# Other starting offsets for the six split-weight buffers of a decoder block

## The chip, the cores and the metric

One core of a Trainium2 chip runs the whole layer in one launch. The metric is the device time of one execution in microseconds (us); before the change the median of three runs is 985.9 us (984.83 to 986.01).

## What is computed

One decoder layer on 512 tokens of width 1024, in float32. Cut to what matters here:

```python
z = rmsnorm(h, g_mix) @ w_in                      # 1024 -> 7168: q, k, v, u, two gates
attn_d = dilated_attention(q, k, v) @ w_attn_proj # 12 heads of 128 in three groups
y = gelu(s5_ssm(u, ...))
ssm_d = (y @ w_glu_a) * sigmoid(y @ w_glu_b)
h = h + (gate_attn * attn_d + gate_ssm * ssm_d) @ w_out
n2 = rmsnorm(h, g_ffn)
h = h + (silu(n2 @ w_ffn_gate) * (n2 @ w_ffn_up)) @ w_ffn_down   # 2816 wide
h = h + sigmoid(h @ w_ple_gate) * (p @ w_ple_proj)
out = rmsnorm(h, g_final)
```

## The kernel before

Every large product is made of three TensorE matmuls on float32r operands. A weight w is split into a high part (`whi`, the value rounded to float32r) and a low part (`wlo`, what is left), an activation likewise, and `mm3` (L312 to L316) issues high by high (L314), high by low (L315) and low by high (L316). In a matmul one operand is loaded into the array first (the stationary one, `lhsT`, at most 128 columns; the profile has this load as PEld) and the other is streamed past it (the moving one, `rhs`, up to 512 columns).

The weights come in 162 chunks of up to 128 x 1024 floats, in a fixed order (`PLAN`, then the merge, output, FFN and final projections). `Weights.dma` loads chunk i into one of four `raw` buffers. `Weights.split` (L192) takes it from there: ScalarE casts it into `whi` (L204), VectorE subtracts to get `wlo` (L205), and the loads are topped up. There are three `whi` and three `wlo` buffers of 1024 floats per partition in the pool `wpool`, taken in turn, so chunk i uses buffer i mod 3; the last four chunks have four buffers each of their own in the pool `L6`. `gemm` (L318) goes over the k blocks of a chunk and calls the next split after its fourth block.

In most products the weights are stationary (128 x 128) and an activation tile of 512 columns moves: `xn` (normalised input), then `at` and `yt` (attention and state-space outputs), `mT` (merged), `h1g` (FFN input), `act` (FFN middle). In the others the weights move and the activation is stationary: the v projections (chunks 0, 1, 6, 7 and 34 to 37, with `xn`, 256 columns), `pp` (chunks 136 and 137, with `pT`, 512 columns) and `pg` (chunks 154 to 161, with `h2`, 256 columns).

Order of work: input transposes and v; then the `w_in` products with the attention and state-space work of VectorE, ScalarE and GpSimd woven between them; merge (`at`, `yt`); output projection (`mT`); the two FFN halves, each `h1g` then `act`; the final gate `pg` with the last normalisation.

Where the tiles begin, in bytes from the start of a partition, as the built program has it, with the remainder by 64 in brackets:

| tile | before |
|---|---|
| `whi` buffers 0, 1, 2 | 42432 [0], 46528 [0], 50624 [0] |
| `wlo` buffers 0, 1, 2 | 54720 [0], 58816 [0], 62912 [0] |
| `xn`, `mT`, `h2` (one place) | 67008 [0] |
| `h1g` | 103872 [0] |
| `at` | 126400 [0] |
| `pT` | 140736 [0] |
| `act` | 159712 [32] |
| `yt` | 174048 [32] |

The parts of a tile that one matmul takes lie 512, 1024 or 2048 bytes apart, so the remainder holds for all of them. By 512, `whi`, `wlo`, `xn`, `mT`, `h2`, `h1g`, `at` and `pT` all have the remainder 448, and `act` and `yt` 480.

Of the kernel before, what the change touches and what calls it, by code (L numbers as in the profile page):

```python
# [11 lines left out]
F32R = mybir.dt.float32r  # L12
# [5 lines left out]
P = 128  # L18
# [17 lines left out]
SLOT = 1024  # L36
# [42 lines left out]
def kernel(  # L79
# [21 lines left out]
    class Engine:  # L101


        def __init__(self, eng, fixed, per, per1):
            self.eng, self.fixed, self.per, self.per1 = eng, fixed, per, per1
            self.free, self.func = 0.0, None
# [49 lines left out]
    def nm(s):  # L156
        uid[0] += 1
        return f"{s}_{uid[0]}"
# [11 lines left out]
    keys = []  # L170
    RAW_BUFS, HL_BUFS = 4, 3

    class Weights:
        def __init__(self):
            self.raw = {}
# [16 lines left out]
        def split(self):  # L192
            i = self.ns
            self.ns += 1
            while self.nd <= i:
                self.dma()
            _, nk, n = chunks[i].shape
            sz = nk * n
            t = self.raw.pop(i)
            end = i >= len(chunks) - 4  # L200
            wp = L6 if end else wpool
            hi = wp.tile([P, SLOT], F32R, tag="whi", name=nm("whi"), bufs=4 if end else HL_BUFS)
            lo = wp.tile([P, SLOT], F32R, tag="wlo", name=nm("wlo"), bufs=4 if end else HL_BUFS)
            sca.copy(hi[:, :sz], t[:, :sz])  # L204
            dve.tensor_sub(lo[:, :sz], t[:, :sz], hi[:, :sz].bitcast(F32))  # L205
            self.hl[i] = tuple(w[:, :sz].rearrange("p (k n) -> p k n", n=n) for w in (hi, lo))
            while self.nd < min(i + 1 + RAW_BUFS, len(chunks)):
                self.dma()
# [1189 lines left out]
```

## Time and profile before

| | |
|---|---|
| median of three runs | 985.9 us (984.83 to 986.01) |
| the profiled execution | 984.2 us, of which its span is 982.4 us |
| mean granted TensorE clock | 0.977 |
| PE busy | 938.5 us (96%), 4764 matmuls |
| PEld busy (weight loads) | 796.7 us (81%) |
| DVE, ACT, POOL busy | 553.3, 318.1, 267.6 us |
| DMA | 97.91 MB, mean 100 GB/s |

Busy time of PE counts modelled ends of pipelined matmuls. How fast TensorE goes is therefore read from the distance between the starts of neighbouring matmuls, not from their durations, and a stage in which PE never sits idle is paced by those distances.

### The profile page before, as it was taken

What the parts mean: (1) busy time and instruction counts of PE and PEld (TensorE: products, weight loads), DVE (VectorE), ACT (ScalarE), POOL (GpSimd) and SP (SyncE); (2) the same over time, 40 slices, a digit from 0 to 9 for tenths busy, and PEclk for the clock granted to TensorE, in tenths of its full rate; (3) what the DMA queues carried; (4) which work ended last, traced back from release to release, by engine and by line L of the source; (5) the groups of instructions that cost most, each with busy time, mean ns of one, the idle gap of its engine ahead of it and who ended that gap; (6) DMA issues with size and microseconds to landing.
All of it is one profiled execution on the core that took longest, in us unless ns stands there. A gap on an engine that the chain in (4) does not pass through costs nothing.

```text
span 982.4 us, 12129 instructions
## 1 busy us (share of the span) xinstructions
PE 938.5 (96%) x4764; PEld 796.7 (81%) x4764; DVE 553.3 (56%) x800; ACT 318.1 (32%) x461; POOL 267.6 (27%) x341
## 2 busy tenths in 40 slices
PE   8798969998999999999999999999999999999995
PEld 8687858777889888888888888888888888888895
DVE  6757887886756577345667543343333444334465
ACT  4432214323422323433333332332222233332343
POOL 3759964963710100100025211110001111100025
PEclk9899979999999999999999999999999999999998
DMA  8656323343243235223343233223343322233302
GB/s 225 189 153 84 87 65 81 77 98 83 84 114 86 66 90 168 86 95 98 86 127 109 86 108 107 86 62 100 96 129 97 96 86 88 60 110 108 115 15 86
DMA packets 172984, 97.91 MB, mean 100 GB/s; under 512 B 20544, under 2 KB 168160, under 8 KB 172928
## 3 DMA queue, kind: packets, MB, share of 16 engines
q1 hardware_dynamic: 161840, 91.34, 32.6%
q10 hardware_dynamic: 10752, 4.76, 2.3%
q0 software_dynamic: 336, 1.05, 0.3%
q8 instruction: 37, 0.61, 0.3%
q14 instruction: 19, 0.16, 0.1%
HBM read 90.34 MB, written 6.78 MB: 99 GB/s over the span
## 4 chain that ended last, share of the span: by engine, by line
PE 67%; DVE 3%; POOL 2%; ACT 2%; DMA 1%; issue 1%; ACTq 0%; DVEq 0%; POOLq 0%
PE mm L314 16%; PE mm L316 16%; PE mm L315 16%; PE aux L314 6%; PE aux L316 6%; PE aux L315 6%; PE aux L306 2%; DMA Bp<-ks 1%; POOL fst L121 1%; PE aux L310 1%; DVE sg L121 1%; DVE late L121 1%; ACT jk L121 1%; POOL mx L121 0%; DVE wlo L121 0%
## 5 line engine op out<-in xcount | busy, mean ns | idle before, releaser
L121 DVE TENSOR_TENSOR wlo<-raw,whi 128x1024 fp32r<-128x1024 f32 (+2 forms) x162 | 196.8, 1218 | 157.6 <-ACT whi L121 156.6
L121 ACT CAST whi<-raw 128x1024 fp32r<-128x1024 f32 (+2 forms) x162 | 160.3, 995 | 216.8 <-PE mm L315 112.4
L314 PE MATMUL mm<-xn,whi 128*128 128x512 f32 x384 | 155.2, 404 | 0.0
L316 PE MATMUL mm<-xn,wlo 128*128 128x512 f32 x384 | 152.2, 396 | 3.0 <-DVE wlo L121 3.0
L315 PE MATMUL mm<-xn,whi 128*128 128x512 f32 x384 | 152.0, 396 | 0.0
L121 POOL TENSOR_TENSOR tg<-tg,tu 128x512 f32<-128x512 f32 x22 | 28.3, 1285 | 273.8 <-DVE tu L121 262.4
L316 PEld LDWEIGHTS mm<-xn,wlo 128*128 128x128 f32 x384 | 73.5, 191 | 19.5 <-DVE wlo L121 3.7
L314 PEld LDWEIGHTS mm<-xn,whi 128*128 128x128 f32 x384 | 74.0, 193 | 14.7 <-issue 0.2
L315 PEld LDWEIGHTS mm<-xn,whi 128*128 128x128 f32 x384 | 73.8, 192 | 14.4
L314 PE MATMUL mm<-act,whi 128*128 128x512 f32 x176 | 69.5, 395 | 0.0
L316 PE MATMUL mm<-act,wlo 128*128 128x512 f32 x176 | 69.5, 395 | 0.0
L315 PE MATMUL mm<-act,whi 128*128 128x512 f32 x176 | 69.5, 395 | 0.0
L314 PE MATMUL mm<-h1g,whi 128*128 128x512 f32 x176 | 68.9, 392 | 0.0
L314 PE MATMUL aux<-h1g,whi 128*128 128x512 f32 x176 | 68.6, 390 | 0.0
L316 PE MATMUL mm<-h1g,wlo 128*128 128x512 f32 x176 | 68.5, 389 | 0.0
L315 PE MATMUL mm<-h1g,whi 128*128 128x512 f32 x176 | 68.5, 389 | 0.0
L316 PE MATMUL aux<-h1g,wlo 128*128 128x512 f32 x176 | 68.5, 389 | 0.0
L315 PE MATMUL aux<-h1g,whi 128*128 128x512 f32 x176 | 68.5, 389 | 0.0
L121 DVE TENSOR_TENSOR tu<-aux,rs 128x512 f32<-128x512 f32 x22 | 15.2, 691 | 57.4 <-PE aux L316 57.4
L121 ACT CAST act<-tg 128x512 fp32r<-128x512 f32 x22 | 13.7, 621 | 90.6 <-POOL tg L121 90.6
L121 DVE TENSOR_TENSOR act<-tg,act 128x512 fp32r<-128x512 f32 x22 | 15.2, 693 | 47.6 <-ACT act L121 47.6
L121 ACT ACT_TABLE_LOAD x21 | 26.9, 1283 | 41.0 <-PE aux L306 20.1
(243 smaller groups left out, 1869.9 us busy)
## 6 DMA issues: line engine op xcount, KB each, us to landing
raw<-in_w_in_dram SPq DMA_DIRECT2D x56, 512.0 KB, 3.8
raw<-in_w_ffn_gate_dram SPq DMA_DIRECT2D x22, 512.0 KB, 3.8
raw<-in_w_ffn_up_dram SPq DMA_DIRECT2D x22, 512.0 KB, 3.9
raw<-in_w_ffn_down_dram SPq DMA_DIRECT2D x16, 384.0 KB, 3.5
raw<-in_w_ffn_down_dram SPq DMA_DIRECT2D x16, 320.0 KB, 3.3
raw<-in_w_out_dram SPq DMA_DIRECT2D x8, 512.0 KB, 4.6
raw<-in_w_ple_gate_dram SPq DMA_DIRECT2D x8, 512.0 KB, 3.5
xT_d<-xTs SPq DMA_DIRECT2D x4, 512.0 KB, 6.3
```

Of the source, the lines that this page charges most:

```text
L121: return fn(dst, *args, **kw)
L306: nc.tensor.matmul(ps, lhsT=lhsT, rhs=rhs, start=start, stop=stop)
L310: nc.tensor.transpose(ps, src, ident[:n, :n])
L314: nc.tensor.matmul(ps, lhsT=lh, rhs=rh, start=start, stop=False)
L315: nc.tensor.matmul(ps, lhsT=lh, rhs=rl, start=False, stop=False)
L316: nc.tensor.matmul(ps, lhsT=ll, rhs=rh, start=False, stop=stop)
```

## The change

Each buffer is 64 floats longer, each of the six has a tag of its own with one buffer in place of a tag with three, and the part of it that is used begins at another offset: 0, 4 and 8 floats into the three `whi`, 64, 32 and 16 floats into the three `wlo`. The four pairs of `L6` follow the same table by i mod 3.

```diff
+    HOMES = ((0, 64), (4, 32), (8, 16))
...
-            hi = wp.tile([P, SLOT], F32R, tag="whi", name=nm("whi"), bufs=4 if end else HL_BUFS)
-            lo = wp.tile([P, SLOT], F32R, tag="wlo", name=nm("wlo"), bufs=4 if end else HL_BUFS)
+            hb, lb = ("whi", "wlo") if end else (f"whi{i % 3}", f"wlo{i % 3}")
+            hi = wp.tile([P, SLOT + 64], F32R, tag=hb, name=nm("whi"), bufs=4 if end else 1)
+            lo = wp.tile([P, SLOT + 64], F32R, tag=lb, name=nm("wlo"), bufs=4 if end else 1)
+            ho, lw = HOMES[i % 3]
+            hi, lo = hi[:, ho:], lo[:, lw:]
             sca.copy(hi[:, :sz], t[:, :sz])
             dve.tensor_sub(lo[:, :sz], t[:, :sz], hi[:, :sz].bitcast(F32))
```

On every engine the instructions, their order, their shapes and the semaphores they wait for are the same in both programs; only addresses differ. Where the used part of each tile begins now:

| tile | after |
|---|---|
| `whi` buffers 0, 1, 2 | 42432 [0], 51152 [16], 59872 [32] |
| `wlo` buffers 0, 1, 2 | 47040 [0], 55616 [0], 64256 [0] |
| `xn`, `mT`, `h2` | 68544 [0] |
| `h1g`, `at`, `pT` | 105408 [0], 127936 [0], 142272 [0] |
| `act`, `yt` | 159712 [32], 174048 [32], as before |

The `raw` buffers stay where they were. By 512, `whi` has the remainders 448, 464 and 480, `wlo` 448, 320 and 256; the activation tiles keep 448 and 480.

## Rows read from the trace of the kernel before

**Rows 1.** Stretches: length, busy us of PE, PEld, DVE, ACT, POOL, clock, DMA, GB/s
```profile
0.00:30.00 30.00, 22.98 (x153) 22.02 (x153) 18.20 (x22) 14.11 (x21) 14.33 (x17) 0.94 0.92 243
...
60.00:110.00 50.00, 46.98 (x257) 40.62 (x256) 33.98 (x75) 15.34 (x23) 41.81 (x105) 0.97 0.52 101
...
260.00:370.00 110.00, 108.17 (x651) 95.85 (x650) 70.91 (x111) 32.09 (x40) 17.00 (x14) 1.00 0.33 93
...
480.00:720.00 240.00, 240.00 (x1056) 196.85 (x1055) 114.90 (x138) 69.78 (x88) 37.11 (x31) 1.00 0.34 98
...
800.00:930.00 130.00, 130.00 (x598) 107.37 (x597) 50.85 (x61) 40.43 (x56) 6.43 (x5) 1.00 0.32 98
```
**Rows 2.** The same view for PE alone, in the last product (`pg`) and v stretches
```profile
297.30:303.10 5.80, 5.80 (x50) 1.00 0.34 93
306.80:325.00 18.20, 18.20 (x155) 1.00 0.30 87
850.00:860.90 10.90, 10.90 (x50) 1.00 0.12 35
922.60:971.60 49.00, 49.00 (x414) 1.00 0.16 54
```
**Rows 3.** Who waited for whom, PE, longest first: us in total, times, longest
```profile
PE aux L306 <- ACT v L121: 12.5, 2, 9.8
...
PE mm L316 <- DVE wlo L121: 3.0, 1, 3.0
```
**Rows 4.** Timeline of PE, FFN, `h1g` moving: start, duration; first and last of 97
```profile
599.76 0.39 PE L314 MATMUL aux<-h1g,whi 128*128 128x512 f32 x1
599.99 0.39 PE L315 MATMUL aux<-h1g,whi 128*128 128x512 f32 x1
600.22 0.39 PE L316 MATMUL aux<-h1g,wlo 128*128 128x512 f32 x1
...
621.52 0.39 PE L314 MATMUL aux<-h1g,whi 128*128 128x512 f32 x1
```
**Rows 5.** Instructions reading `act`, first FFN half: duration min/median/max, first and last start
```profile
L314 PE MATMUL mm<-act,whi x88: 393/396/399, 667.8 to 728.7; 128*128 128x512 f32 x88
L315 PE MATMUL mm<-act,whi x88: 393/394/397, 668.0 to 728.9; 128*128 128x512 f32 x88
L316 PE MATMUL mm<-act,wlo x88: 393/396/397, 668.2 to 729.1; 128*128 128x512 f32 x88
```
**Rows 6.** Timeline of PE, v projection, weights moving: first and last of 48
```profile
297.32 0.28 PE L314 MATMUL mm<-whi,xn 128*128 128x256 f32 x1
...
302.95 0.28 PE L316 MATMUL mm<-whi,xn 128*128 128x256 f32 x1
```
**Rows 7.** Weight loads by tile, two products: duration min/median/max, first and last start
```profile
L316 PEld LDWEIGHTS mm<-h1g,wlo x176: 187/188/188, 546.9 to 844.2; 128*128 128x128 f32 x176
...
L316 PEld LDWEIGHTS mm<-act,wlo x176: 187/187/188, 668.0 to 922.1; 128*128 128x128 f32 x176
```
**Rows 8.** Timeline of PE, transposes whose stationary tile begins at remainder 32, then 0
```profile
179.62 1.03 PE L310 MATMUL aux<-cst,Bp 128*128 128x128 f32 x8
...
225.82 0.60 PE L310 MATMUL aux<-cst,vT 128*128 128x128 f32 x4
```
**Rows 9.** Groups by form, DVE, then ACT: count, busy us, mean ns, idle before
```profile
L121 DVE TENSOR_TENSOR wlo<-raw,whi 128x1024 fp32r<-128x1024 f32 x130 | 168.4, 1298 | 117.1 <-ACT whi L121 116.4
...
L121 DVE TENSOR_TENSOR act<-tg,act 128x512 fp32r<-128x512 f32 x22 | 15.2, 693 | 47.6 <-ACT act L121 47.6
...
L121 DVE TENSOR_TENSOR h<-h1T,h 128x512 fp32r<-128x512 f32 x8 | 5.5, 692 | 5.5 <-ACT h L121 5.5
...
L121 ACT CAST act<-tg 128x512 fp32r<-128x512 f32 x22 | 13.7, 621 | 90.6 <-POOL tg L121 90.6
...
L121 ACT CAST h<-h1T 128x512 fp32r<-128x512 f32 x8 | 5.0, 622 | 29.2 <-DVE h1T L121 29.2
```

## The prediction

> **What bounds the kernel now.** I read the busy time by stretch first. From about 260 us on TensorE is busy in all or nearly all of every stretch (108.17 of 110, 240.00 of 240, 130.00 of 130 us) at a granted clock of 1.00, its upper level of 2.4 GHz [rows 1]; before that it shares the bound with the other engines (22.98 of the first 30 us, 46.98 of the 50 from 60 us on). Who waits for whom comes second: the largest total that PE waits for anything is 12.5 us, for an attention tile, and a split weight made it wait once, 3.0 us [rows 3]. So neither loads nor splits pace this kernel; the distance between the starts of neighbouring matmuls does, and I read that third, from start times. With `h1g` moving, 96 steps go from 599.76 to 621.52 us: 226.7 ns each [rows 4]. With `act` moving, 87 steps of three matmuls go from 667.8 to 728.7 us: 60.9 us / 261 = 233.3 ns [rows 5]. With weights moving at 256 columns, 47 steps go from 297.32 to 302.95 us: 119.8 ns [rows 6]. The difference between 512 and 256 columns, 106.9 ns, is 0.4176 ns a column, one column per cycle of 2.4 GHz; what is left over is about 13 ns per matmul at either width.
>
> The `act` step is the row to look at. The shape, the weight buffers and the engine's freedom are the same as with `h1g`, yet each matmul takes 6.6 ns more, which is 16 cycles, or 64 bytes of float32 at a column a cycle. What differs in the map of the built program is the start of the moving tile: `act` begins 32 bytes past a multiple of 64, `h1g` on one. My reading: **a moving operand that starts inside a 64-byte line pays for one line more.** Its 2048 bytes then lie in 33 lines and not 32.
>
> **The change, part by part.** No instruction is added, removed or moved on any engine, and no wait. Only addresses change, so the sum is made of steps of TensorE that get longer or shorter, and of splits that might.
>
> *Weights as the moving operand.* `whi` buffers 1 and 2 now begin at remainder 16 and 32. They move in L314 and L316 (high weights in two of three matmuls). Eleven chunks of 256 columns are concerned: chunk 1, chunk 7, chunks 34, 35 and 37, and six of the eight chunks of `pg` (156 and 159 use buffer 0), with 32 such matmuls each: 352. The two `pp` chunks, 512 columns wide, add 16 each: 32. Together 384. No 256-column row with a start inside a line exists in the trace. The bounds are 0 (the row of [rows 6], 119.8 ns, as if nothing changed) and 6.6 ns ([rows 5] against [rows 4]); below nothing is excluded for this term, since these operands start on a line now. I take 6.6 ns, because the left-over of 13 ns is the same at both widths, so the extra line should be too.
>
> What of it shows: in the `pg` stretch PE is busy in 49.00 of 49.00 us, in the late v stretches in 5.80 of 5.80 and 18.20 of 18.20, in `pp` in 10.90 of 10.90 [rows 2]. Those 192 + 96 + 32 = 320 matmuls pay in full: 2.1 us. Chunks 1 and 7 lie where PE also waits for others [rows 1]: 64 matmuls, between 0 and 0.4 us; I take half. Sum: **+2.3 us** (2.1 to 2.5).
>
> *Weights as the stationary operand.* 1,416 matmuls now load a `whi` that begins at remainder 16 or 32 (512 with `xn`, 464 with `h1g`, 80 with `mT`, 64 with `at`, 232 with `act`, 64 with `yt`). The load is recorded at 187 to 188 ns beside a moving stream of 226.7 or 233.3 ns [rows 7]. Nearest row for a stationary tile off a line: eight transposes of `Bp` (start at remainder 32) take 1.03 us from the first start to the last end, four of `vT` (remainder 0) 0.60 us [rows 8]; the difference is four steps, 0.43 us, or 108 ns each, which is also the step of `vT` alone ((0.60 - 0.27) / 3, a transpose's duration being 0.27 us). At a step half as long as here the start of the stationary tile costs nothing, so I take 0. The upper bound is one line, 6.6 ns x 1,416 = 9.4 us.
>
> *Moving activations.* `xn`, `mT`, `h2`, `h1g`, `at` and `pT` shift by 1536 bytes and keep their remainder; `act` and `yt` stay put. Cost 0.
>
> *The splits.* ACT casts into `act` (remainder 32) in 621 ns and into `h2` (remainder 0) in 622 ns; DVE's subtraction takes 693 and 692 ns [rows 9]. Starts do not matter to them. Were a split slower by some per cent, DVE idles 117 us before its wide splits [rows 9], and PE waited for one only once. Cost 0; if that cover were gone, PE's waits for `wlo` would grow from 3.0 us [rows 3].
>
> Against the profiled execution (984.2 us) the sum gives 986.5 us. The median of the runs shown is 1.7 us above that execution, 985.9 us, so the forecast is **988.2 us**, with 987.5 to 989.0 for this case alone: the ends 2.1 and 2.5 us of the sum and half a microsecond of scatter.
>
> **A page against a row.** The Trainium skill, page "SBUF — State Buffer", section "Specifications (TRN2)", says that SBUF has lines of 16 bytes and that only crossing into a new line costs. By it a start at 16 or 32 bytes would be as good as one at 64, and the sum would be 0, the first rival below. The trace disagrees as far as it reaches: `act` starts on a multiple of 16 and pays 6.6 ns [rows 5]. The section "Who interferes with whom" of the same page gives TensorE two independent read ports, and says it never waits for another reader; by that rule distances between weights and activations are worth nothing, in either direction, and the trace agrees, since the step is the same over all the distances it has among aligned tiles.
>
> **The rivals.** *Nothing happens.* The extra line may be hidden at 256 columns, or the odd starts may not count at 16 bytes. For it: no row of this trace shows that case. Against: the same left-over at both widths. Time: 985.9 us plus at most the `pp` matmuls, 32 x 6.6 ns = 0.2 us; scatter of the runs is 1.2 us from lowest to highest.
>
> *The distance counts, against the change.* In this trace every stationary tile of a float32r matmul starts on a line, so the `act` penalty may also come from the distance between moving and stationary operand, modulo 64. Then 1,120 matmuls on aligned activations with `whi` 1 or 2 begin to pay, 122 of `act` with `whi` 2 stop paying, and the 384 pay too: 1,382 x 6.6 ns = 9.1 us, 995.0 us. If the stationary start costs a line of its own on top of the forecast, it is 9.4 + 2.3 us, 997.6 us. For it: the rows cannot tell it from my reading. Against: [rows 8], and the constant step across three lines of `mm3` with different pairs.
>
> *The distance counts, for the change.* All distances on the aligned tiles are multiples of 512 bytes. Were the 13 ns left over per matmul a collision of the weight load with the stream, it would go where the distance changes: buffers 1 and 2, two thirds of 4,032 matmuls. All of it would be 2,688 x 13 ns = 35 us, 951 us; half of it 968 us. It decides as soon as one stage on `xn` or `h1g` steps below 226.7 ns in two chunks of three. Against: the one other distance in the trace, 32 bytes off, is slower, not faster [rows 5]. The Trainium skill, page "TensorE: Matmul & The Clock Gate", section "Wait — 56ns, not 53.3ns?", states a step of 215.7 ns for 512 columns at full clock, 11 ns below the row; if that whole gap were collision, this rival's estimate by the page would be 29 us. The trace has no step that short.
>
> **How the numbers follow.** One line more for moving weights: 0.55. Nothing: 0.16. Distance or stationary start against the change: 0.14. Distance for it: 0.09. Something else, of either sign: 0.06. About 0.2% of the time, 2 us, is what a measurement of this kernel can tell from no change. The forecast is just over that; with the scatter I give 0.7 of its chance to slower and 0.3 to no difference. Slower: 0.39 + 0.14 + 0.03 = 0.56. Same: 0.16 + 0.16, and little else, 0.33. Faster: 0.09 + 0.02 = 0.11. The range leaves out the gain and the dearest case: 984.8 (nothing, at the lowest run seen) to 995.5 (distance modulo 64, with scatter).
>
> **What would show it.** Right: the `pg` step near 126 ns for `whi` moving in buffers 1 and 2 and 120 ns in buffer 0; `wlo` moving (L315) at 120 ns in all; `h1g` still 226.7 ns and `act` 233.3 ns with every buffer; the gap between 922 and 972 us longer by 1.3 us. Wrong: `h1g` steps that change with the chunk modulo 3 (distance or stationary start, by the sign), `pg` at 120 ns throughout (nothing), or longer splits on ACT or DVE.

## The result and the profile after

The changed kernel is **slower**, by 0.6%: 991.9 us median against 985.9 us of the kernel before, 13 runs each, ratio 1.0058 with a 95% interval of 1.0041 to 1.0075. One of the 13 executions of the changed kernel took 1328.8 us at a granted clock of 0.653, and the ratio leaves it out. The forecast was 988.2 us and its wide range, 984.8 to 995.5 us, held the time; the narrow one for its likeliest case, 987.5 to 989.0 us, did not. The term of the forecast was not what cost the time, and a rival that had 0.14 was nearer.

The profiled execution of the changed kernel took 989.0 us, its span 987.1 us, 4.7 us more than the span of before. Its page begins:

```profile
span 987.1 us, 12129 instructions
## 1 busy us (share of the span) xinstructions
PE 943.2 (96%) x4764; PEld 794.1 (80%) x4764; DVE 550.7 (56%) x800; ACT 317.8 (32%) x461; POOL 267.8 (27%) x341
```

The work is the same, and of the engines TensorE alone is busy clearly longer, by 4.7 us. The splits did not change, as forecast, and PE waited for one of them once, 3.0 us, as in [rows 3] (the view of who waits for whom, after):

```profile
PE mm L321 <- DVE wlo L121: 3.0, 1, 3.0
```

These are the groups by form of DVE and ACT, after, which answer to [rows 9]:

```profile
L121 DVE TENSOR_TENSOR wlo<-raw,whi 128x1024 fp32r<-128x1024 f32 x130 | 168.8, 1302 | 118.7 <-ACT whi L121 118.0
...
L121 ACT CAST act<-tg 128x512 fp32r<-128x512 f32 x22 | 13.7, 621 | 93.0 <-POOL tg L121 93.0
```

Where the stages begin tells where the time went. First the matmuls that read a tile, kernel before (count, duration min/median/max in ns, first and last start in us); the row for `act` is in [rows 5]:

```profile
L314 PE MATMUL mm<-mT,whi x64: 388/389/402, 502.9 to 546.0; 128*128 128x512 f32 x64
...
L314 PE MATMUL mm<-h1g,whi x176: 389/389/478, 546.7 to 844.0; 128*128 128x512 f32 x176
...
L314 PE MATMUL aux<-whi,pT x16: 389/389/389, 850.1 to 860.3; 128*128 128x512 f32 x16
...
L314 PE MATMUL mm<-whi,h x128: 278/283/363, 922.6 to 971.6; 128*128 128x256 f32 x128
```

The same after, the row for `act` cut to the first FFN half (L314 to L316 are now L319 to L321):

```profile
L319 PE MATMUL mm<-mT,whi x64: 389/392/398, 503.1 to 546.8; 128*128 128x512 f32 x64
...
L319 PE MATMUL mm<-h1g,whi x176: 389/393/477, 547.5 to 848.6; 128*128 128x512 f32 x176
...
L319 PE MATMUL mm<-act,whi x88: 387/395/401, 670.8 to 731.4; 128*128 128x512 f32 x88
...
L319 PE MATMUL aux<-whi,pT x16: 388/397/398, 854.8 to 865.3; 128*128 128x512 f32 x16
...
L319 PE MATMUL mm<-whi,h x128: 276/282/370, 927.3 to 975.9; 128*128 128x256 f32 x128
```

From `mT` to the first `h1g` it is 43.8 us before and 44.4 after; from there to `act` 121.1 and 123.3; from `act` over the second `h1g` to `pT` 182.3 and 184.0; from `pT` to `pg` 72.5 both times; `pg` itself, first to last start, 49.0 and **48.6**. The stage that was to pay 1.3 us became 0.4 us shorter. From the first `mT` on, the loss sits in the stages where an aligned activation (one that begins on a multiple of 64) moves and the weights are *stationary*: 0.6 + 2.2 + 1.7 = 4.5 us. Up to `mT`, at about 503 us, the two executions differ by only 0.2 us. But their granted clocks differ as well (mean over the span 0.977 before, 0.983 after; 0.78 and 0.89 from 30 to 60 us), so this pair does not show what the change cost there. How the loss is spread within a stage the timeline of PE shows, after, at four neighbouring chunks of `h1g` (24 matmuls each; rows are the first matmul of a chunk):

```profile
587.65 0.39 PE L319 MATMUL aux<-h1g,whi 128*128 128x512 f32 x1
...
593.21 0.40 PE L319 MATMUL mm<-h1g,whi 128*128 128x512 f32 x1
...
598.68 0.39 PE L319 MATMUL aux<-h1g,whi 128*128 128x512 f32 x1
...
604.27 0.39 PE L319 MATMUL mm<-h1g,whi 128*128 128x512 f32 x1
```

The chunks use buffers 2, 0 and 1 and take 5.56, 5.47 and 5.59 us, or 231.7, 227.9 and 232.9 ns a step, where it was 226.7 ns with all three [rows 4]. Buffer 0 keeps the distance that it had by 512, and of its chunk only the first seven steps differ (225 to 236 ns); from there on the step is 226.7 ns again. The step changes with the chunk modulo 3: what the prediction had written down as the sign of a distance, or a stationary start, that counts.

### The profile page after: what moved, and what is told of

Its sections match the earlier page's. It is cut to its first block, busy times and chain, and to the rows that moved or that the text cites. A ratio compares the mean times of both kernels' runs of the same rounds, so it can differ in the third digit from the quotient of the medians.

```text
span 987.1 us, 12129 instructions
## 1 busy us (share of the span) xinstructions
PE 943.2 (96%) x4764; PEld 794.1 (80%) x4764; DVE 550.7 (56%) x800; ACT 317.8 (32%) x461; POOL 267.8 (27%) x341
## 4 chain that ended last, share of the span: by engine, by line
PE 68%; DVE 3%; POOL 2%; ACT 2%; DMA 1%; issue 1%; ACTq 0%; POOLq 0%; DVEq 0%
PE mm L319 16%; PE mm L320 16%; PE mm L321 16%; PE aux L319 6%; PE aux L320 6%; PE aux L321 6%; PE aux L311 2%; DMA Bp<-ks 1%; POOL fst L121 1%; PE aux L315 1%; DVE late L121 1%; DVE sg L121 1%; ACT jk L121 1%; POOL mx L121 0%; DVE wlo L121 0%
## 5 line engine op out<-in xcount | busy, mean ns | idle before, releaser
L319 PE MATMUL mm<-xn,whi 128*128 128x512 f32 x384 | 155.7, 406 | 0.2 <-ACT vt L121 0.2
L321 PE MATMUL mm<-xn,wlo 128*128 128x512 f32 x384 | 152.8, 398 | 3.0 <-DVE wlo L121 3.0
L321 PEld LDWEIGHTS mm<-xn,wlo 128*128 128x128 f32 x384 | 73.5, 191 | 20.9 <-DVE wlo L121 3.8
L319 PEld LDWEIGHTS mm<-xn,whi 128*128 128x128 f32 x384 | 73.5, 191 | 15.5 <-ACT vt L121 0.5
L319 PE MATMUL mm<-h1g,whi 128*128 128x512 f32 x176 | 69.7, 396 | 0.0
L319 PE MATMUL aux<-h1g,whi 128*128 128x512 f32 x176 | 69.4, 394 | 0.0
L319 PE MATMUL mm<-act,whi 128*128 128x512 f32 x176 | 69.4, 394 | 0.0
L321 PE MATMUL mm<-act,wlo 128*128 128x512 f32 x176 | 69.2, 393 | 0.0
L321 PE MATMUL aux<-h1g,wlo 128*128 128x512 f32 x176 | 69.1, 393 | 0.0
L321 PE MATMUL mm<-h1g,wlo 128*128 128x512 f32 x176 | 69.1, 393 | 0.0
```

What stands on the lines that cost most here:

```text
L319: nc.tensor.matmul(ps, lhsT=lh, rhs=rh, start=start, stop=False)
L321: nc.tensor.matmul(ps, lhsT=ll, rhs=rh, start=False, stop=stop)
```

## The experiments

Two theories beside the forecast's reading (*moving start alone*) go through all of them: that the distance between the moving and the stationary operand (how far apart they begin in a partition) counts, by its remainder by 64 or by a larger number, and that the stationary start alone counts.

### The same places, one offset for all (k1_same)

```diff
-    HOMES = ((0, 64), (4, 32), (8, 16))
+    HOMES = ((0, 64), (0, 64), (0, 64))
```

> The buffers keep the change's length and interleaved places, but every split weight begins at the remainder 448 by 512, like the activations. Distance by 64 and moving start alone: both give back the kernel before, 985.9 us, h1g steps 226.7 ns with all three buffers. Distance by 512 (multiples of 64 count too): the same, since all distances are multiples of 512 again. Place (the interleaving, the 1536 bytes of shift): stays near the change, 991 us, and the steps with buffer 0 stay as they are after the change (first steps of a chunk 231 to 236 ns).

Measured: 985.6 us, ratio 1.0002 (0.9982 to 1.0022). Two rows of PE's timeline, 60 steps apart:

```profile
586.73 0.39 PE L320 MATMUL mm<-h1g,whi 128*128 128x512 f32 x1
...
600.33 0.39 PE L320 MATMUL aux<-h1g,whi 128*128 128x512 f32 x1
```

13.60 us / 60 = 226.7 ns, over chunks of all three buffers. Longer buffers, a tag for each, other places and a shift of the activations by 1536 bytes cost nothing within the interval (about 2 us either way), and the step is that of before; the offsets cost it all.

### Only the high, only the low parts (k2_hi, k3_lo)

```diff
-    HOMES = ((0, 64), (4, 32), (8, 16))
+    HOMES = ((0, 64), (4, 64), (8, 64))
```

for the high parts, and for the low parts

```diff
-    HOMES = ((0, 64), (4, 32), (8, 16))
+    HOMES = ((0, 64), (0, 32), (0, 16))
```

> Only the high parts begin at 0, 16 and 32 bytes; all low parts at a distance of a multiple of 512 from the aligned activations. Distance by 64 (or stationary start): all of the loss stays, 991 to 992 us, steps with whi 1 at about 233 ns and with whi 2 at about 231 ns on h1g. Distance by 512: a part of it, 988 to 990 us, since the low parts' 64, 128 and 192 bytes are gone. Moving start alone: 988.2 us, h1g at 226.7 ns.

> Only the low parts differ, by multiples of 64 bytes; all high parts lie at multiples of 512 from the aligned activations. Distance by 64, stationary start, moving start: none of the loss, 985.9 us, h1g 226.7 ns throughout. Distance by 512: about a third to a half of it, 988 to 989 us, with h1g steps over 230 ns where a low part of buffer 1 or 2 is loaded.

Measured: ratio 1.0030 (1.0013 to 1.0048) with the high parts alone, 1.0051 (1.0028 to 1.0074) with the low parts alone. Both cost. Their sum would be 1.0081 against the change's 1.0058, and the intervals are too wide to tell these apart; that the two do not add shows in the steps. The chunks of `h1g` in the order of buffers 2, 0, 1, first matmul of each, high parts alone:

```profile
588.87 0.39 PE L319 MATMUL aux<-h1g,whi 128*128 128x512 f32 x1
...
594.43 0.39 PE L319 MATMUL mm<-h1g,whi 128*128 128x512 f32 x1
...
599.89 0.39 PE L319 MATMUL aux<-h1g,whi 128*128 128x512 f32 x1
...
605.33 0.39 PE L319 MATMUL mm<-h1g,whi 128*128 128x512 f32 x1
```

and low parts alone:

```profile
588.23 0.39 PE L319 MATMUL aux<-h1g,whi 128*128 128x512 f32 x1
...
593.77 0.39 PE L319 MATMUL mm<-h1g,whi 128*128 128x512 f32 x1
...
599.23 0.39 PE L319 MATMUL aux<-h1g,whi 128*128 128x512 f32 x1
...
604.77 0.39 PE L319 MATMUL mm<-h1g,whi 128*128 128x512 f32 x1
```

High parts: 5.56 us with the one 32 bytes off, but 5.44 us, the time of before, with the one 16 bytes off. Low parts: 5.54 us with either of those that lie 192 and 128 bytes off by 512, though they begin on a multiple of 64. The chunk of buffer 2 takes 5.56 us with the high parts moved, 5.54 us with the low parts and 5.56 us with both, so one cost does not come on top of the other. The remainder by 64 is not the rule, and a stationary tile that begins off a multiple of 64 is not needed for the loss. Moving start alone fails both runs: with the high parts its 988.2 us is met (988.5 us), but by luck, since it has `h1g` at 226.7 ns throughout, and `h1g` lost.

### All weights 32 bytes further (k6_w32)

```diff
     wpool = ctx.enter_context(tc.tile_pool(name="wpool", bufs=1))
+    wpool.tile([P, 8], F32, name="wpad")
...
     apool = ctx.enter_context(tc.tile_pool(name="apool", bufs=1))
+    apool.tile([P, 8], F32, name="apad")
```

(in the kernel before; the second pad puts the activations back on a multiple of 64, `act` and `yt` stay; the buffers of the last four chunks move by 64 bytes and keep their distance)

> The kernel before with all raw and split buffers of the weights 32 bytes further and the aligned activations where they were by 64, act and yt untouched. Distance by 64: h1g, xn, mT, at rise towards 231 to 233 ns, act and yt fall to 226.7 ns; 2,496 steps up and 720 down by about 5 ns: +9 us, 995 us. Moving start alone: h1g 226.7 and act 233.3 ns as before, time 986 to 989 us. Stationary start alone: h1g up as with distance, act stays at 233 ns or higher; 998 us.

Measured: ratio 1.0074 (1.0050 to 1.0097), about 7 us. The steps swap. Timeline of PE, `h1g` moving, 96 steps apart, then the instructions that read `act` in the first half:

```profile
599.13 0.39 PE L317 MATMUL aux<-h1g,whi 128*128 128x512 f32 x1
...
621.53 0.39 PE L317 MATMUL aux<-h1g,whi 128*128 128x512 f32 x1
```

```profile
L316 PE MATMUL mm<-act,whi x88: 389/389/395, 671.7 to 730.9; 128*128 128x512 f32 x88
```

`h1g`, which still begins on a multiple of 64, now takes 22.40 us / 96 = 233.3 ns; `act`, which nobody moved, takes 59.2 us / 261 = 226.8 ns, though now both it and the weights begin 32 bytes off. This is the run that decides. Neither the start of the moving tile nor that of the stationary one sets the step, **the distance between them does**. The 9 us expected lie within the interval (4.9 to 9.6 us).

### A sweep of distances (sweep)

```python
for d in list(range(0, 512, 16)) + [512, 1024, 1536, 2048, 2064, 2080]:
    ps = bank()
    for rep in range(4):
        for k in range(8):
            nc.tensor.matmul(ps, lhsT=w128(d, k), rhs=X[:, k], start=..., stop=...)
```

(`w128(d, k)` is 128 columns of a weight tile, d bytes and k times 512 bytes from its start; the tile's distance from `X` is a multiple of 512)

> None of the layer is computed: only float32r matmuls on one moving tile and one weight tile, both 32 bytes past a multiple of 64. First part: 512 columns, stationary operand at a distance of 0, 16, ... 496 bytes (then 512 to 2080) from the moving tile by 512, 32 matmuls for each. Distance by 64: a step that repeats every 64 bytes, 226.7 ns at 0 and 233.3 ns at 32. Distance by 512 (64-byte multiples count too): 226.7 ns at 0 only, and again at 512, 1024 and 2048. Relation of successive operands, and no constant distance but 32: 226.7 ns at every multiple of 64 here, since in this part all matmuls of a group have the same distance, while the second part, where one matmul in three has a distance of its own, shows steps of 230 to 236 ns wherever the two distances differ, as in the run with only the low parts moved. Third part: weights moving at 256 columns, 119.8 ns at 0, below it at some of 16, 32, 48 as in the changed kernel (117 to 118 ns).

Each row is a merged stretch of PE's timeline: its start, the time to the end of its last matmul, and how many matmuls it holds. First 512 columns, at 16, 32, 64, 240, 256 and 512 bytes:

```profile
26.29 5.60 PE L115 MATMUL mm<-X,W 128*128 128x512 f32 x24
...
33.59 5.76 PE L115 MATMUL mm<-X,W 128*128 128x512 f32 x24
...
48.52 5.76 PE L115 MATMUL mm<-X,W 128*128 128x512 f32 x24
...
130.73 5.38 PE L115 MATMUL mm<-X,W 128*128 128x512 f32 x23
...
137.76 5.60 PE L115 MATMUL mm<-X,W 128*128 128x512 f32 x24
...
256.48 5.60 PE L115 MATMUL mm<-X,W 128*128 128x512 f32 x24
```

With 0.39 us for the last one, 5.60 us is (5.60 - 0.39) / 23 = 226.5 ns, 5.76 us is 233.5 ns and 5.38 us over 22 steps is 226.8 ns. Over all 38 distances the step settles at 226.7 ns where the distance is 0, 16 or 240 by **256**, and is 230 to 234 ns everywhere else, at 64, 128 and 192 too (means over the last 23 steps of a group; the group at 0, with which the kernel starts, steps about 427 ns for its first dozen matmuls, and 226 to 227 ns over its last 16). The rule by 64 falls, and so does that by 512: the pattern repeats after 256 bytes. That both tiles begin 32 bytes past a multiple of 64 does not keep the step from 226.7 ns. The relation of successive operands is no better a rule by itself, since 64 is slow with one distance throughout.

In the second part the third matmul of each three has a distance of its own. Each row holds six threes and one matmul more; the distances are 0 with 16, 0 with 32, 16 with 16 and 32 with 32:

```profile
304.75 4.47 PE L122 MATMUL mm<-X,W 128*128 128x512 f32 x19
...
310.20 4.59 PE L122 MATMUL mm<-X,W 128*128 128x512 f32 x19
...
349.18 4.60 PE L122 MATMUL mm<-X,W 128*128 128x512 f32 x19
...
399.25 4.60 PE L122 MATMUL mm<-X,W 128*128 128x512 f32 x19
```

Three steps take (4.47 - 0.39) / 6 = 680 ns at 0 with 16, as at 0 with 0, and (4.59 - 0.39) / 6 = 700 ns at 0 with 32, within the rounding of a row as much as with all three at 32. The other pairs lie between 688 and 706 ns. So **one matmul in three at another distance can cost as much as three**. This fits that the low parts alone cost about what both cost, and that `act` kept 233.1 ns a step with buffer 2 of the changed kernel, whose high part lies at distance 0 from it and whose low part lies at 32. The pairs 16 with 16 and 16 with 0 take 700 ns, where the first part has 226.7 ns a step at 16: at 16 bytes the short step is not certain. The groups at 16 of the first part each ran right after one at a multiple of 256, and these two did not; that this decides was not tried by itself.

The third part, weights moving at 256 columns, at 0, 64 and 192 bytes:

```profile
521.88 3.16 PE L129 MATMUL mm<-W,X 128*128 128x256 f32 x25
...
537.00 3.00 PE L129 MATMUL mm<-W,X 128*128 128x256 f32 x25
...
567.12 3.00 PE L129 MATMUL mm<-W,X 128*128 128x256 f32 x25
```

(3.16 - 0.28) / 24 = 120.0 ns at 0 and 113.3 ns at 64 and 192. Here 0 is about the slowest distance. That `pg` got shorter with the change, which took the weights of buffers 1 and 2 off 0, fits this; the runs with `h2` and v below try it.

### act and yt at distance 0 (k5_act0)

```diff
                 R = ctx.enter_context(tc.tile_pool(name="R", bufs=1, side="right"))
+                R.tile([P, 8], F32, name="rpad")
```

> The kernel before with a pad of 32 bytes ahead of the tiles on the right side, so that act and yt too begin at remainder 448 by 512, like all the others. Any form of the distance theory, and moving start too: act and yt steps fall from 233.3 to 226.7 ns, 720 x 6.6 ns = 4.8 us faster than before, 981 us (ratio 0.995). If the higher step of act and yt is tied to their place or their later use, nothing: 985.5 us.

Measured: 980.5 us, ratio **0.9954 (0.9938 to 0.9970)**, 4.7 us faster where 4.8 were expected. The row that answers to [rows 5]:

```profile
L314 PE MATMUL mm<-act,whi x88: 389/389/390, 667.4 to 726.6; 128*128 128x512 f32 x88
```

59.2 us / 261 = 226.8 ns. One pad of 32 bytes beats both kernels.

### Distances for the moving weights (k7_h2, k8_v, k9_all)

```diff
-    h2 = apool.tile([P, 2, KD, T], F32R, tag="A", name="h2")
+    h2 = apool.tile([P, 2 * KD * T + 64], F32R, tag="A", name="h2")[:, 16:16 + 2 * KD * T].rearrange(...)
```

(`xn` and `mT`, which share its place, get the same length) and for the v chunks

```diff
-            hi = wp.tile([P, SLOT], F32R, ...)
+            hi = wp.tile([P, SLOT + 64], F32R, ...)
...
+            off = 16 if keys[i] == "v" else 0
+            hi, lo = hi[:, off:], lo[:, off:]
```

> The kernel before with h2 64 bytes further (its place is 256 bytes longer, so all else keeps its remainder by 256). In pg the weights then move at a distance of 192 by 256 from the stationary h2. Distance by 256, as the sweep's third part has it (113.3 ns at 64, 112 and 192, 119.9 at 0): 384 steps 6.6 ns shorter, 2.5 us faster, 982.7 us, pg steps at 113.3 ns. Moving start alone: h2 is stationary there and starts on a line as before, no change, 985.2 us.

> The kernel before with 64 floats more per split buffer (no remainder by 256 changes) and the v chunks 64 bytes into theirs. Distance by 256: 384 steps of the v projections 6.6 ns shorter, of which the 192 late ones show in full and the early ones in part, 1.3 to 2.5 us faster, 983 to 984 us, late v steps at 113.3 ns. Moving start alone: they start on a line as before, no change, 985.2 us.

> The last two and the pad that puts act and yt at remainder 448 together. Distance by 256, the gains add: 4.7 (measured alone) + 2.5 + 1.3 to 2.5 us, 975.5 to 976.7 us, ratio 0.990 to 0.991. If PE's gain in pg or v is taken by a wait for a split, 978 to 980 us.

Measured: 0.9995 (0.9976 to 1.0013) with `h2` moved, 1.0011 (0.9997 to 1.0025) with the v chunks moved, no difference either time; both of these together with the pad for `act` and `yt` 978.1 us, 0.9939 (0.9918 to 0.9960), whose interval overlaps that of the pad alone. The rows of `pg`, with `h2` moved and with all three edits:

```profile
L314 PE MATMUL mm<-whi,h x128: 276/281/365, 923.6 to 972.0; 128*128 128x256 f32 x128
```

```profile
L316 PE MATMUL mm<-whi,h x128: 281/281/365, 915.2 to 963.6; 128*128 128x256 f32 x128
```

Both take 48.4 us from the first to the last start, 0.6 us less than before, not 2.5. The steps of `pg` with `h2` moved, and of v with the v chunks moved, fell from 119 to 120 ns to 117 to 118 ns and not to the 113.3 ns of the sweep. A gain of 0.6 us is lost within the intervals of these runs. The sweep's order of operands is another than that of `mm3`; that this is the reason was not tried. That `k9_all` is faster than the pad alone is not shown.

## Why the prediction was right and where it was wrong

**What bounds the kernel: right.** No load and no split paced the changed kernel (PE waited for a split once, 3.0 us, as before); the time went where the step of TensorE changed, and DVE and ACT kept theirs.

**That the range held the time is luck as far as the forecast's own term goes.** That term was 2.3 us; the loss is 6 us (4.0 to 7.4 us), and of that term only the 0.2 us of `pp` came about (0.3 us longer, 10.2 to 10.5 us from the first to the last start). The range reached far enough because it took in the price of a rival.

**The step that failed is the reading of the `act` row.** "A moving operand that starts inside a 64-byte line pays for one line more" explained 226.7 against 233.3 ns [rows 4, 5], but the rows could not tell a start from a distance: all stationary tiles in them had the same remainder as `h1g`. The text said so under its rival and gave it 0.14; against it stood [rows 8] and the constant step across the three lines of `mm3`. But the three pairs of those lines all have the same distance by 256, so their constant step could say nothing. Moving the weights and leaving `act` alone took its 6.6 ns away and gave them to `h1g` (k6_w32). With it falls what the prediction says against a start at 16 or 32 bytes: `act`, which starts where it did, steps 226.8 ns there.

**Weights as the moving operand: +2.1 to 2.5 us forecast, a small gain measured in `pg`.** `pg` was to grow by 1.3 us and shrank by 0.4 us. The 256-column case had no row; the left-over of 13 ns at both widths was taken to mean the same rule, and the sweep shows the widths to differ: no distance tried is better than 0 for 512 columns, but several are for 256.

**Weights as the stationary operand: 0 forecast, and here was the loss.** The 0 came from transposes [rows 8], a float32 form with other steps (108 ns), which say nothing on float32r. The upper bound kept there, 9.4 us, was the right one to keep: it and the rival's 9.1 us put 995.5 us into the range, and the measured time, 6 us above before, lies inside.

**Moving activations: 0 forecast, and right** (k1_same), with a shift of 1536 bytes, six times 256; a shift by another amount would have changed the distances.

**The rivals.** Distance against the change was right in kind and gave 995.0 us, 3 us too much; its rule by 64 was too narrow in one way (low parts 128 and 192 bytes away cost, too) and too strict in another (16 bytes off can be free, and `act` gained where it met buffer 1: 60.6 us from the first to the last start in its first half, 60.9 before). Its sum, a price for each matmul at a distance, is not the form of the cost either, as 0 with 32 shows in the sweep. Distance in favour of the change is excluded for 512 columns by the sweep: no multiple of 16 bytes is better than the 0 that the kernel before already had for all but `act` and `yt`. The sentence of the Trainium skill that TensorE's two read ports are independent and that it never waits for another reader ("SBUF — State Buffer", section "Who interferes with whom") was said to agree with the trace; taken as a rule that distances are worth nothing, it does not agree with the run in which all weights moved by 32 bytes and `h1g` went from 226.7 to 233.3 ns. That the step was the same over all distances of aligned tiles was so because all of them were multiples of 512.

What stays open: why the step depends on the distance at all (whether the load of the weights and the stream collide was not tested); why the short step at 16 bytes holds in some sequences and not in others (buffer 1 with only the high parts moved has 16 and 0 and steps 226.7 ns, while the sweep's 16 with 0 takes 700 ns for three); and why `pg` did not reach 113.3 ns. No run separates the distance to a matmul's own stationary tile from that to the next one's, which is loaded meanwhile.

## What to carry to other kernels

Where TensorE is back to back, read the step between starts for each product and compare those of one shape: two values for one shape are a question of where operands lie, and the address map of the program belongs beside the trace. Keep a 512-column float32r product's stationary and moving tiles, high and low parts alike, a multiple of 256 bytes apart, by a pad where a pool's end leaves an odd offset; spreading the offsets made the kernel slower here. If a row can be explained by a position or by a difference of positions, move one of the two operands before believing either.

## What the runs showed of the hardware that was not expected

- The step of 512-column float32r matmuls depends on the distance of stationary and moving operand by 256 bytes: in the sweep, in steps of 16 bytes, 226.7 ns at 0, 16 and 240, 230 to 234 ns elsewhere. Beyond the 213.3 ns of 512 columns at 2.4 GHz (the granted clock was 1.00) that is 13.3 ns at best and 20 ns mostly, 32 and 48 cycles.
- With 256 columns 0 is not the best distance: 113.3 ns at 64, 112 and 192 bytes, 117 to 120 ns elsewhere, 120 ns at 0; that is 16 and 32 cycles above the 106.7 ns of the columns at best and at 0. In the layer's `pg` and v such distances gave 117 to 118 ns.
- It has a memory. In the sweep at 240 bytes the step settles within the first few matmuls (238, 233, 229, 226, 227 ns), and in the changed kernel buffer 0, at distance 0 throughout, needs seven steps after a chunk of buffer 2 to come back to 226.7 ns. At 16 bytes both 226.7 and 233 ns are seen.
- One matmul in three at another distance can cost as much as all three: 700 ns for three steps at 0 with 32 and at 32 with 32, 680 ns at 0 with 0.
